# A four-layer streaming encoder step on one core: costs in the ordering table, side matmuls admitted some time after their estimate, and the rotated-key add moved from GpSimd to VectorE

## The chip, the cores and the metric

One core of one Trainium2 chip runs the whole program. Its engines each take their instructions in one fixed order: TensorE (PE in the profile, with PEld for its weight loads), VectorE (DVE), ScalarE (ACT), GpSimd (POOL) and SyncE (SP), which issues the transfers. The metric is the device time of one execution in microseconds, as the median over several runs.

## The reference

One inference step of a hybrid encoder for 256 frames of a new stream (prompt) and 64 frames of a running one (sample), so 320 columns of work in float32. Four layers in the pattern A, B, C, A:

- A: differential attention, 16 heads. Per head two softmax maps, `p = attn_map(q1, k1) - lam * attn_map(q2, k2)`, the output normalised, q and k rotated (rope). The sample frames also read 512 cached keys.
- B: sparse attention, where an indexer picks the 256 (or fewer) best keys of each query.
- C: RWKV-7 time mixing, a matrix state carried from token to token.

```
x <- x + W_out[i] (mixer(rmsnorm(x)) * silu(gate))
y = rmsnorm(x)
```

Returned beside y are the new keys and values of A and B, the index keys, and the states of C.

## The kernel before

All activations stand with the model dimension on the 128 partitions and the 320 frames along the free axis. Every projection is cut into tiles of 128 output columns; one tile is 48 matmuls of 320 columns: 16 pieces of the inner dimension, each in three products, because every float32 operand is split into two parts of a faster format (hi and lo). The weights come in by SP, are split into a ring of five slots by ACT (hi) and DVE (lo), and are multiplied into a PSUM bank. There are 307 such tiles, 14736 matmuls, called weight matmuls below; in the profile they carry `ring` in their names. The plan of tiles is fixed: layer A takes 64 (per head k, v, q and the gate of the head before), its output projection 16, then B and 16, C (v, two narrow tiles, k and r, then g) and 16, A and 16.

Everything else of a layer (rope, scores, softmax, transposes, products with the values, the recurrence of C) is side work. When a tile is done, a generator such as `on_k`, `on_q`, `attend`, `sample`, `steps` or `chain` is started for it and yields instructions in its own order. All generators, and the ring's `splitter`, are merged when the program is built into one order per engine. `Model` holds an estimated clock for each engine, `cost` gives each instruction an estimated length, and `ready` says when its inputs would be there. `pump` walks the generators and puts out the next instruction of each whose inputs are estimated to be ready by PE's estimated clock. Between any three weight matmuls (one inner piece) the loop at the end of the program calls `pump`, so a side matmul can be let in after each group of three. None of it runs on the chip: what is left is the order. On the chip an engine stops at an instruction whose inputs are late, and all that stands behind it on this engine stops too.

One head of layer A in steady state is four tiles, 192 weight matmuls, with these side groups on PE: the transposes of v (three), the scores of the prompt's rows (three products, from q and k), the scores of the sample (six) and of the last prompt rows (three) in split form, the transposes of the head before's output, those of the sample's map (five) and of the prompt's map (three, in `attend`, after eight exponentials on ACT and two combining instructions on DVE), and the eight products with the values. In `on_k` the rotated key is the sum of two DVE products `t1` and `t2`; the add stands at line 823 for A (32 heads in both layers) and 1278 for B (4), and the sum is stored, sent out, and split for the score products.

In layer C each of 16 tiles p has a `chain`: four prompt steps c0 to c3 (c4 is the sample's, beside them), each of three dependent groups of small matmuls with copies between them, then a normalisation over ACT, DVE and POOL, and three transposes. The result is operand number p of C's output projection, whose weight matmuls need all 16 from the 154th on.

Of the kernel before, what the change touches and what calls it, by code (L numbers as in the profile page):

```python
# [24 lines left out]
RING = 5  # L25
LEAD = 4
ARENA = 18480
NEG = -1.0e30


class Op:


    def __init__(self, eng, name, args, kw):
        self.eng, self.name, self.args, self.kw = eng, name, args, kw
        self.hold = not kw.get("stop", True)
        ins, outs = [], []
        for i, x in enumerate(args):
            if isinstance(x, bass.AP):
                (ins if i else outs).append(x)  # L40
        for k, x in kw.items():
            if isinstance(x, bass.AP):
                (outs if k in ("out", "accum_out") else ins).append(x)
        self.size = max([1] + [x.free_size() for x in ins + outs if name == "dma_start" or not _dram(x)])
        self.psum = any("psum" in x.name for x in ins)
        self.f32r = any(x.dtype == F32R for x in ins)
        self.width = outs[0].partition_size() if outs else 128
        self.bytes = outs[0].nbytes() if outs else 0
        self.run = min((run(x) for x in ins + outs), default=0) if name == "dma_start" else 0
        self.n = outs[0].free_size() if outs else 0  # L50
        self.scalars = sum(x.free_size() == 1 for x in ins) if self.n > 1 else 0
        self.accum = "accum_out" in kw
        self.ins = [region(x) for x in ins if "psum" not in x.name]
        self.outs = [region(x) for x in outs if "psum" not in x.name]
        self.banks = set()
        for x in ins + outs:
            if "psum" in x.name:
                a = int(x.offset) % int(x.ap[0][0])
                b = a + sum(int(st) * (int(n) - 1) for st, n in x.ap[1:])
                self.banks.update(range(a // 512, b // 512 + 1))  # L60
        self.column = int(outs[0].offset) // (outs[0].ap[0][0] or 1) if eng == "PE" else 0


def _dram(x):
    return str(x.space).endswith("DRAM")


def run(x):

    r = 1  # L70
    for st, n in reversed(x.ap if _dram(x) else x.ap[1:]):
        if n > 1 and st != r:
            break
        r *= int(n)
    return r
# [19 lines left out]
class Model:  # L95


    def __init__(self, engines):
        self.engines = engines
        self.clk = {e: 0.0 for e in engines}  # L100
        self.dma = self.hwdge = 0.0
        self.table = None
        self.mem, self.dram = {}, {}
        self.cols = {}
        self.bank = {}
# [27 lines left out]
    def cost(self, op):  # L133
        n = op.size
        if op.name == "dma_start":
            return 1040.0 if op.eng == "G" else 100.0
        if op.eng == "PE":
            n = op.n
            if op.column:
                return 27 if n <= 32 else 54  # L140
            if op.name == "transpose":
                return 0.84 * n
            if op.f32r:
                return 0.42 * n + 2
            return 1.67 * max(n, op.width) + 4
        if op.eng == "S":
            c = 0.714 * n + (90 if op.psum else 132) + 95 * op.scalars + 70 * op.accum
            f = op.args[2] if op.name == "activation" else None
            if f in (AF.Exp, AF.Tanh, AF.Sqrt):
                f = "sqrt" if f == AF.Sqrt else "exp"  # L150
                if f != self.table:
                    c += 1300
                    self.table = f
            return c
        if op.eng == "G":
            if op.kw.get("op") == OP.pow:
                return 165.0 * op.n + 300
            if op.name == "memset":
                return 0.835 * n + 35
            if op.name == "tensor_copy":  # L160
                return 3.33 * n + 120
            if op.name == "tensor_scalar":
                return 3.33 * n + 176 + 83 * op.scalars
            return 2.1 * n + 149
        if op.name == "reciprocal":
            return 6.45 * n + 69
        if op.name in ("tensor_scalar", "tensor_copy", "memset") and not op.psum:
            return 0.52 * n + 69 + 60 * op.scalars
        return 1.042 * n + 69 + 60 * op.scalars
# [38 lines left out]
class Sched:  # L208
# [45 lines left out]
    def pump(self):  # L254

        while True:
            self.moved, nxt = False, None
            for t in list(self.tasks):
                while self.settle(t):
                    n = 1  # L260
                    while t.queue[n - 1].hold:
                        n += 1
                    r = max(self.model.ready(op) for op in t.queue[:n])
                    if r > max(self.now, self.model.clk["PE"]):
                        nxt = r if nxt is None else min(nxt, r)
                        break
                    for op in t.queue[:n]:
                        self.model.emit(op)
                    del t.queue[:n]
                    self.moved = True  # L270
                    self.moves += 1
            if not self.moved:
                return nxt
# [164 lines left out]
def hybrid_kernel(ctx: ExitStack, tc: tile.TileContext, a, o, layers=DEPTH):  # L438
# [3 lines left out]
    PE, V, S, G, Q = [sched.engine(e) for e in ("PE", "V", "S", "G", "Q")]  # L442
# [27 lines left out]
    ring = wpool.tile([128, RING, 2, 512], F32R, name="ring")  # L470
    raw = wpool.tile([128, RAW, 2048], F32, name="raw")
    arena = wpool.tile([128, ARENA], F32, name="arena")
    psum = ppool.tile([128, 4096], F32, name="psum")
# [7 lines left out]
    class Layout:  # L481
# [3 lines left out]
        def ap(self, n):  # L485
            r = arena[:, self.off:self.off + n]
            self.off += n
            assert self.off <= ARENA, self.off
            return r
# [16 lines left out]
    def wait(*keys):  # L506
        while sched.cur.queue or not all(k in flags for k in keys):
            yield
# [220 lines left out]
    def layer_a(j, li, opn, opo, prev):  # L729
# [85 lines left out]
        def on_k(h):  # L815
            def gen(acc):
                yield from wait(("tab", li))
                t1, t2 = yield from TT.get(2)
                yield from rope_parts(t1.ap, t2.ap, acc.ap, cos, sin, 32)
                acc.rel()  # L820
                yield
                kr = yield from KR.get()
                G.tensor_add(kr.ap, t1.ap, t2.ap)
                t1.rel()
                t2.rel()
                flags["k", li, h] = kr
                Q.dma_start(o["new_a_k"][j, h], kr.ap)
                flags["kdone", li, h] = True
            return gen
# [245 lines left out]
    def layer_b(li, opn, opo, prev):  # L1075
# [153 lines left out]
        def topk():  # L1229
# [11 lines left out]
            yield from rounds(acc_p[:, 128:384], 8)  # L1241
            V.tensor_scalar(bias_p, acc_p, -2.5e38, NEG, op0=OP.is_ge, op1=OP.mult)
            flags["bias_p"] = True
            yield
            yield from rounds(acc_s[0:64], 18)
            V.tensor_scalar(bias_s[0:64], acc_s[0:64], -2.5e38, NEG, op0=OP.is_ge, op1=OP.mult)
            V.tensor_copy(bias_s[64:128], bias_s[0:64])
# [22 lines left out]
        def on_k(g):  # L1270
            def gen(acc):
                yield from wait(("tab", li))
                t1, t2 = yield from TT.get(2)
                yield from rope_parts(t1.ap, t2.ap, acc.ap, cosb, sinb, 64)
                acc.rel()
                yield
                kr = yield from KTT.get()
                G.tensor_add(kr.ap, t1.ap, t2.ap)
                t1.rel()
                t2.rel()  # L1280
                Q.dma_start(o["new_b_k"][g], kr.ap)
                flags["bk", g] = kr
            return gen
# [216 lines left out]
    def layer_c(li, opo, prev):  # L1500
# [18 lines left out]
        mts = {}  # L1519
        top = arena[:, ARENA - 2 * T:ARENA]  # L1520
        tw, ta = top[:, 0:T], top[:, T:2 * T]
# [8 lines left out]
        LL, XT, VS, VK = lv.slots(6, T), lv.slots(8, T), lv.slots(4, T), lv.slots(2, 640)  # L1530
        assert lv.off <= ARENA - 2 * T

# [106 lines left out]
        WL, VV = lk.slots(2, 512), lk.slots(2, T)  # L1639
        batch_at = ARENA - 2 * T - 2304  # L1640
        LG = Layout(batch_at - 4 * T).slots(4, T)
# [232 lines left out]
        SG = lg.slots(1, T)  # L1874
        assert ARENA - 2 * T <= lg.off - T and lg.off <= ARENA, lg.off
        SETS = Slots(sched, sets[0:3])
# [370 lines left out]
    for n, p in enumerate(pieces):  # L2247
# [13 lines left out]
        for i in range(4):  # L2261
# [6 lines left out]
            r = max(model.ready(x) for x in ops)  # L2268
            while True:
                nxt = sched.pump()  # L2270
                t = max(sched.now, model.clk["PE"])
# [127 lines left out]
```

## Time and profile before

| | us |
|---|---|
| median of 3 runs (2772.8 to 2778.11) | 2776.75 |
| the profiled execution | 2782.14 |
| its span, first to last instruction | 2780.3 |
| PE busy, of the span | 2702.5 |
| DVE / ACT / POOL busy | 1929.8 / 1466.2 / 467.0 |

PE is busy 97% of the span, but its records overlap (matmuls are pipelined), so the share hides short stops. A stop is read from the start times: the weight matmuls of a tile follow each other at a fixed pitch, and what lies between two of them beyond that pitch is side work or waiting. The profile puts nearly all instructions on line 198, the helper that emits them, so tiles and shapes tell them apart: `psum<-op_a,ring` or `psum<-op_b,ring` are weight matmuls, `psum<-cst,arena` are transposes, `psum<-arena` scores and products. An fp32 product of two arena operands has two records.

### The profile page before, as it was taken

The page shows a single profiled execution, that of the slowest core. Times are in us where ns is not written, and L with a number is a line of the kernel's source. Part 1 is how long each engine was busy: PE and PEld are TensorE (multiplying, and loading weights), DVE is VectorE, ACT ScalarE, POOL GpSimd, SP SyncE. Part 2 cuts the span into 40 slices and gives each one's busy share as a digit, 9 for nine tenths or more (in the row PEclk, how much of TensorE's full clock was granted, in tenths as well). Part 3 has the DMA queues.
Part 4 walks back from the last instruction along what each step waited for, and adds up shares of the span by engine and source line. Part 5 has one row for each costly group of instructions (what it writes and reads, how often), then busy time and mean ns, then how long its engine had stood idle before and what let it go on. Part 6 is the DMA issues. An engine that isn't in the chain of part 4 may idle for free.

```text
span 2780.3 us, 53272 instructions
## 1 busy us (share of the span) xinstructions
PE 2702.5 (97%) x19594; PEld 2573.0 (93%) x19594; DVE 1929.8 (69%) x4044; ACT 1466.2 (53%) x3582; POOL 467.0 (17%) x845
## 2 busy tenths in 40 slices
PE   7999999999999999989999999999999999999997
PEld 7999999999999999989999998888899999999997
DVE  7777777665799766458866667766656777777654
ACT  5655555554444544436544453667545555555553
POOL 3000000001000000022012635455311000000011
PEclk9999999999999999989999999999999999999999
DMA  6444444455434334565666676766454444444352
GB/s 219 150 143 142 141 143 145 141 173 187 142 127 149 119 131 140 189 175 180 228 180 203 172 206 174 256 219 196 149 193 149 146 146 146 147 145 148 131 174 104
DMA packets 219980, 455.23 MB, mean 164 GB/s; under 512 B 83270, under 2 KB 149254, under 8 KB 185798
## 3 DMA queue, kind: packets, MB, share of 16 engines
q1 hardware_dynamic: 219718, 451.83, 49.8%
q8 instruction: 154, 2.52, 0.4%
q14 instruction: 108, 0.88, 0.1%
HBM read 394.20 MB, written 57.55 MB: 162 GB/s over the span
## 4 chain that ended last, share of the span: by engine, by line
PE 44%; ACT 4%; DVE 3%; issue 2%; DMA 1%; POOL 0%; SPq 0%; DVEq 0%; ACTq 0%; POOLq 0%
PE psum L198 44%; ACT arena L198 3%; DVE arena L198 1%; DVE ring L198 1%; ACT ring L198 1%; DVE smt L198 1%; DMA arena<-yr_d 0%; DMA bv_d<-arena 0%; DMA arena<-l_d 0%; DVE op_a L198 0%; POOL arena L198 0%; DMA yr_d<-arena 0%; DMA v_d<-arena 0%; SPq L198 0%; DVE op_b L198 0%
## 5 line engine op out<-in xcount | busy, mean ns | idle before, releaser
L198 PE MATMUL psum<-op_a,ring 128*128 128x320 f32 x8496 | 1329.1, 313 | 20.3 <-ACT op_a L198 10.0
L198 PEld LDWEIGHTS psum<-op_a,ring 128*128 128x128 f32 x8496 | 1260.9, 189 | 34.9 <-ACT op_a L198 11.9
L198 DVE TENSOR_TENSOR ring<-raw,ring 128x512 fp32r<-128x512 f32 (+2 forms) x1228 | 856.8, 702 | 512.2 <-ACT ring L198 499.2
L198 ACT CAST ring<-raw 128x512 fp32r<-128x512 f32 (+2 forms) x1228 | 751.7, 618 | 834.1 <-PE psum L198 770.0
L198 PE MATMUL psum<-op_b,ring 128*128 128x320 f32 (+1 forms) x6240 | 996.6, 314 | 0.3 <-DVE ring L198 0.2
L198 PEld LDWEIGHTS psum<-op_b,ring 128*128 128x128 f32 (+1 forms) x6240 | 923.4, 188 | 17.4 <-issue 3.0
L198 DVE TENSOR_TENSOR arena<-psum,arena 32x320 f32<-32x320 f32 (+3 forms) x567 | 270.0, 476 | 82.7 <-PE psum L198 64.2
L198 PE MATMUL psum<-arena 128*64 128x64 f32 (+9 forms) x3428 | 302.7, 254 | 8.9 <-DVE arena L198 4.0
L198 PEld LDWEIGHTS psum<-arena 128*64 128x64 f32 (+4 forms) x3428 | 239.8, 147 | 63.8 <-issue 31.2
L198 POOL TENSOR_TENSOR arena<-arena 128x64 f32<-128x64 f32 (+18 forms) x254 | 179.6, 710 | 654.4 <-PE psum L198 240.4
L198 ACT COPY arena<-psum 64x128 f32<-64x128 f32 (+9 forms) x473 | 146.0, 332 | 133.5 <-PE psum L198 116.8
L198 ACT ACTIVATE arena<-psum,smt 64x576 f32<-64x576 f32 (+5 forms) x384 | 169.7, 443 | 72.4 <-PE psum L198 35.1
L198 PE MATMUL psum<-cst,arena 128*128 128x128 f32 (+3 forms) x807 | 133.0, 269 | 26.6 <-DVE arena L198 20.9
L198 PEld LDWEIGHTS psum<-cst,arena 128*128 128x128 f32 (+3 forms) x807 | 89.0, 135 | 65.2 <-issue 26.3
L198 POOL TENSOR_TENSOR smt<-smt,mhalf 128x3 f32<-128x3 f32 (+1 forms) x64 | 72.7, 1136 | 310.2 <-DVE smt L198 296.9
L198 POOL TENSOR_TENSOR ssum<-ssum,arena 128x320 f32<-128x320 f32 x70 | 64.6, 923 | 294.8 <-ACT arena L198 294.1
L198 POOL MEMSET smt<- 128x3 f32 (+2 forms) x85 | 8.3, 102 | 609.1 <-DVE smt L198 609.1
L198 ACT CAST op_b<-arena 128x320 fp32r<-128x320 f32 (+4 forms) x198 | 79.1, 417 | 49.3 <-DVE arena L198 27.1
L198 ACT ACTIVATE arena<-arena 128x320 f32<-128x320 f32 (+1 forms) x192 | 89.4, 473 | 29.0 <-DVE arena L198 17.6
L198 DVE TENSOR_TENSOR op_b<-arena,op_b 128x320 fp32r<-128x320 f32 (+4 forms) x198 | 91.7, 483 | 5.0 <-ACT op_b L198 4.8
L198 ACT CAST op_a<-arena 128x320 fp32r<-128x320 f32 (+2 forms) x136 | 59.3, 442 | 55.6 <-DVE arena L198 35.9
L198 DVE TENSOR_TENSOR arena<-arena 64x320 f32<-64x320 f32 (+13 forms) x207 | 83.8, 414 | 3.4 <-DMA arena<-l_d 0.5
(95 smaller groups left out, 1366.5 us busy)
## 6 DMA issues: line engine op xcount, KB each, us to landing
raw<-in_a_w_in_dram SPq DMA_DIRECT2D x120, 1024.0 KB, 5.0
raw<-in_c_w_rkvg_dram SPq DMA_DIRECT2D x52, 1024.0 KB, 5.4
raw<-in_w_out_dram SPq DMA_DIRECT2D x48, 1024.0 KB, 5.1
raw<-in_b_w_in_dram SPq DMA_DIRECT2D x45, 1024.0 KB, 4.9
raw<-in_w_out_dram SPq DMA_DIRECT2D x64, 256.0 KB, 3.6
arena<-rec_d SPq DMA_DIRECT2D x16, 962.5 KB, 5.2
raw<-in_c_w_rkvg_dram SPq DMA_DIRECT2D x48, 256.0 KB, 3.8
out_dram<-arena SPq DMA_DIRECT2D x72, 160.0 KB, 4.3
```

The costliest lines, as they stand in the source:

```text
L198: return getattr(self.engines[op.eng], op.name)(*op.args, **op.kw)
```

## The change

Five numbers or rules of the ordering, and two adds:

- ScalarE instructions with an accumulated sum are estimated 50 ns longer (120 for 70). GpSimd's power is estimated at 157 ns a column and 390 (165 and 300 before), its other two-input work at 2.3 ns a column (2.1).
- `SLACK`: `pump` treats a PE instruction of a generator as ready 400 ns after its estimate. Weight matmuls have no such addition.
- The rotated keys' add is issued on VectorE, in A and in B.
- `Op` and `Model` get some new fields that nothing reads.

```
+SLACK = 400.0
...
-            c = 0.714 * n + (90 if op.psum else 132) + 95 * op.scalars + 70 * op.accum
+            c = 0.714 * n + (90 if op.psum else 132) + 95 * op.scalars + 120 * op.accum
...
-                return 165.0 * op.n + 300
+                return 157.0 * op.n + 390
...
-            return 2.1 * n + 149
+            return 2.3 * n + 149
...
-                    r = max(self.model.ready(op) for op in t.queue[:n])
+                    r = max(self.model.ready(op) + (SLACK if op.eng == "PE" else 0.0) for op in t.queue[:n])
...
-                G.tensor_add(kr.ap, t1.ap, t2.ap)
+                V.tensor_add(kr.ap, t1.ap, t2.ap)
...
-                G.tensor_add(kr.ap, t1.ap, t2.ap)
+                V.tensor_add(kr.ap, t1.ap, t2.ap)
```

How it moves instructions is seen in the built order. First PE, in one steady head of the first layer A, from the sample's last transpose to the weight matmuls ahead of the next head's scores, before:

```order
L198 MATMUL psum<-cst,arena 64x64
L198 MATMUL psum<-op_a,ring 128x320 x24
L198 MATMUL psum<-cst,arena 128x128 x3
L198 MATMUL psum<-op_a,ring 128x320 x9
L198 MATMUL psum<-arena 128x128 x3
L198 MATMUL psum<-arena 64x128 x5
L198 MATMUL psum<-op_a,ring 128x320 x45
L198 MATMUL psum<-cst,arena 128x128 x2
L198 MATMUL psum<-cst,arena 64x128
L198 MATMUL psum<-op_a,ring 128x320 x72
```

And the same stretch in the changed kernel:

```order
L209 MATMUL psum<-cst,arena 64x64
L209 MATMUL psum<-op_a,ring 128x320 x27
L209 MATMUL psum<-cst,arena 128x128
L209 MATMUL psum<-op_a,ring 128x320 x3
L209 MATMUL psum<-cst,arena 128x128 x2
L209 MATMUL psum<-op_a,ring 128x320 x12
L209 MATMUL psum<-arena 128x128 x3
L209 MATMUL psum<-arena 64x128 x5
L209 MATMUL psum<-op_a,ring 128x320 x36
L209 MATMUL psum<-cst,arena 128x128 x2
L209 MATMUL psum<-cst,arena 64x128
L209 MATMUL psum<-op_a,ring 128x320 x72
```

The map's three transposes come after 27 weight matmuls (the first) and 30 (the other two) in place of 24, and the products with the values after 42 in place of 33. Counted from the program's start by the numbers behind the x, the transposes of v stand 12 weight matmuls into their tile (9 before), and the scores 36 (33 before).

Second PE, at the end of layer C, the last groups of chain 15 and what follows. Before: its step c3 (three groups), then its transposes:

```order
L198 MATMUL psum<-arena 64x64 x2
L198 MATMUL psum<-op_a,ring 128x320 x6
L198 MATMUL psum<-arena 64x64 x2
L198 MATMUL psum<-op_a,ring 128x320 x12
L198 MATMUL psum<-arena 64x64 x2
L198 MATMUL psum<-arena 64x128
L198 MATMUL psum<-arena 64x64 x2
L198 MATMUL psum<-op_a,ring 128x320 x57
L198 MATMUL psum<-cst,arena 128x128 x2
L198 MATMUL psum<-cst,arena 128x64
L198 MATMUL psum<-op_a,ring 128x320 x615
```

In the changed kernel c3 of chain 15 is one block (the second to the fourth row here); then come chain 14's transposes, three weight matmuls, and chain 15's transposes:

```order
L209 MATMUL psum<-op_a,ring 128x320 x18
L209 MATMUL psum<-arena 64x64 x6
L209 MATMUL psum<-arena 64x128
L209 MATMUL psum<-arena 64x64 x2
L209 MATMUL psum<-cst,arena 128x128 x2
L209 MATMUL psum<-cst,arena 128x64
L209 MATMUL psum<-op_a,ring 128x320 x3
L209 MATMUL psum<-cst,arena 128x128 x2
L209 MATMUL psum<-cst,arena 128x64
L209 MATMUL psum<-op_a,ring 128x320 x615
```

Chain 15's last step moved from 57 weight matmuls ahead of its transposes to 3 ahead of them.

Third VectorE, in the first layer A, from the split of the next cached keys on. Before, no row of these is the key's add (it stands on POOL):

```order
L198 TENSOR_TENSOR op_b<-arena,op_b 128x512
L198 TENSOR_TENSOR ring<-raw,ring 128x512
L198 TENSOR_TENSOR arena<-psum,arena 64x128
L198 TENSOR_TENSOR op_b<-arena,op_b 128x320
L198 TENSOR_TENSOR ring<-raw,ring 128x512
L198 TENSOR_SCALAR smt<-smt 128x3
L198 TENSOR_TENSOR ring<-raw,ring 128x512
L198 TENSOR_TENSOR arena<-psum,smt 128x256
L198 TENSOR_SCALAR arena<-arena,smt 64x128
L198 TENSOR_TENSOR arena<-psum,rstd 128x320
```

In the changed kernel:

```order
L209 TENSOR_TENSOR arena<-arena 128x320
L209 TENSOR_TENSOR op_b<-arena,op_b 128x512
L209 TENSOR_TENSOR ring<-raw,ring 128x512
L209 TENSOR_TENSOR arena<-psum,arena 64x128
L209 TENSOR_TENSOR op_b<-arena,op_b 128x320
L209 TENSOR_TENSOR ring<-raw,ring 128x512
L209 TENSOR_SCALAR smt<-smt 128x3
L209 TENSOR_TENSOR arena<-psum,rstd 128x320
L209 TENSOR_TENSOR ring<-raw,ring 128x512
L209 TENSOR_TENSOR arena<-psum,smt 128x256
```

The add is the first row, ahead of the cached keys' split; and the product that v's transposes read (`psum,rstd`) now stands ahead of the one that waits for POOL's power (`psum,smt`).

## Rows read from the trace of the kernel before

**Rows 1.** The page, part 1: busy time and share of each engine.
```profile
PE 2702.5 (97%) x19594; PEld 2573.0 (93%) x19594; DVE 1929.8 (69%) x4044; ACT 1466.2 (53%) x3582; POOL 467.0 (17%) x845
```

**Rows 2.** Stretches: length, busy PE, PEld, DVE, ACT, POOL, granted clock, DMA share, GB/s.
```profile
60.00:580.00 520.00, 510.15 (x3502) 483.11 (x3500) 375.38 (x820) 306.03 (x817) 39.96 (x91) 1.00 0.42 143
1480.00:1758.00 278.00, 267.51 (x1785) 254.15 (x1783) 190.20 (x334) 123.19 (x248) 127.27 (x194) 0.97 0.71 201
1758.00:1990.00 232.00, 230.91 (x2780) 192.26 (x2780) 158.78 (x372) 152.56 (x544) 123.24 (x259) 1.00 0.60 191
...
1987.00:1995.00 8.00, 6.09 (x30) 5.44 (x30) 4.53 (x8) 1.92 (x4) 0.93 (x2) 0.82 0.79 262
```

**Rows 3.** PE in order, one head of layer A: start, length, operation, count [idle before].
```profile
2200.02 10.80 PE L198 MATMUL psum<-op_b,ring 128*128 128x320 f32 x72
...
2211.64 0.73 PE L198 MATMUL psum<-op_b,ring 128*128 128x320 f32 x3
...
2213.01 2.36 PE L198 MATMUL psum<-op_b,ring 128*128 128x320 f32 x15
2215.21 0.52 PE L198 MATMUL psum<-op_a 128*128 128x256 f32 x3
...
2220.24 3.79 PE L198 MATMUL psum<-op_b,ring 128*128 128x320 f32 x24
2224.35 0.81 PE L198 MATMUL psum<-cst,arena 128*128 128x128 f32 x3 [0.32 <-DVE arena L198]
2224.91 1.56 PE L198 MATMUL psum<-op_b,ring 128*128 128x320 f32 x9
...
2228.02 6.86 PE L198 MATMUL psum<-op_b,ring 128*128 128x320 f32 x45
...
2235.23 10.07 PE L198 MATMUL psum<-op_b,ring 128*128 128x320 f32 x67
```

**Rows 4.** PE in order, where scores and transposes find their inputs ready.
```profile
2138.06 2.90 PE L198 MATMUL psum<-op_b,ring 128*128 128x320 f32 x18
...
2141.44 1.62 PE L198 MATMUL psum<-op_b,ring 128*128 128x320 f32 x9
...
2161.84 2.90 PE L198 MATMUL psum<-op_b,ring 128*128 128x320 f32 x18
...
2164.82 5.38 PE L198 MATMUL psum<-op_b,ring 128*128 128x320 f32 x35
```

**Rows 5.** DVE in order, same head, ahead of the map's transposes.
```profile
2222.06 0.18 DVE L198 RECIPROCAL smt<-smt 128x4 f32<-128x4 f32 x1 [2.43 <-ACT arena L198]
...
2223.85 0.74 DVE L198 SCALAR_TENSOR_TENSOR arena<-arena,smt 128x128 f32<-128x128 f32 x2
```

**Rows 6.** Groups by shape, 60 to 580 us, the last 760 to 1120: count, busy, mean ns.
```profile
L198 POOL TENSOR_TENSOR arena<-arena 128x320 f32<-128x320 f32 x14 | 16.8, 1202 | 115.5 <-ACT arena L198 44.6 <-PE psum L198 39.8 <-DVE arena L198 31.1
L198 DVE TENSOR_TENSOR arena<-arena 64x320 f32<-64x320 f32 x30 | 14.5, 483 | 0.5
L198 DVE TENSOR_TENSOR op_b<-arena,op_b 128x512 fp32r<-128x512 f32 x13 | 14.4, 1105 | 0.2 <-ACT op_b L198 0.2
...
L198 DVE TENSOR_TENSOR op_b<-arena,op_b 128x512 fp32r<-128x512 f32 x2 | 1.4, 689 | 0.0
```

**Rows 7.** PE in order, end of layer C.
```profile
1975.70 0.34 PE L198 MATMUL psum<-arena 128*64 128x64 f32 x4
...
1979.26 0.79 PE L198 MATMUL psum<-arena 128*64 128x64 f32 x10
1979.98 8.62 PE L198 MATMUL psum<-op_a,ring 128*128 128x320 f32 x57
1988.49 0.61 PE L198 MATMUL psum<-cst,arena 128*128 128x128 f32 x3
1990.89 9.37 PE L198 MATMUL psum<-op_a,ring 128*128 128x320 f32 x49 [1.79 <-ACT op_a L198]
```

**Rows 8.** DVE in order, chain 15's last product ahead of its transposes.
```profile
1987.11 1.24 DVE L198 TENSOR_TENSOR arena<-arena,smt 128x384 f32<-128x384 f32 x1 [0.35 <-POOL smt L198]
```

More of the change, by code (lines that the diff above doesn't have):

```diff
@@ L61, in __init__ @@
         self.column = int(outs[0].offset) // (outs[0].ap[0][0] or 1) if eng == "PE" else 0
+        self.mode = self.place = None
+        if eng == "PE":
+            self.mode = ins[0].partition_size() > 64, self.width > 64
+        elif outs and not _dram(outs[0]):
+            self.place = self.column if eng == "PE" else int(outs[0].offset) // (outs[0].ap[0][0] or 1), self.width
+        self.weights = any("ring" in x.name for x in ins)
+        self.pair = eng == "V" and not self.psum and sum(x.free_size() > 8 for x in ins) > 1
+        self.pool = eng == "G" and name.startswith("tensor_") and sum(x.free_size() > 32 for x in ins) > 1
 def _dram(x):
@@ L102, in __init__ @@
         self.table = None
+        self.last = {}
+        self.pool = (0.0, 0.0)
         self.mem, self.dram = {}, {}
```

## Prediction

> **What bounds the kernel now.** I read the busy shares first: PE is busy 97% of the span, no other engine over 69% [rows 1]. So time can only come from PE, and the question is how much of its busy time is work. The stretches by stage come next: PE is idle for 9.9 of 520 us in the first layer A, for 10.5 of 278 us in the second part of C, and for 1.1 of 232 us while C's chains run [rows 2]. Since a PE record also covers waiting inside it, I then read PE's order in time in one steady head of A and take differences of start times. Fifteen weight matmuls take 2215.21 - 2213.01 = 2.20 us, a pitch of 0.1467 us [rows 3]. A side group costs what lies between the weight matmuls around it beyond that pitch:
>
> - The map's transposes: 24 weight matmuls start at 2220.24, the next ones at 2224.91: 4.67 - 24 x 0.1467 = 1.15 us [rows 3].
> - The transposes of v: 45 from 2228.02, next at 2235.23: 7.21 - 6.60 = 0.61 us [rows 3].
> - The scores: 72 from 2200.02, next at 2211.64: 11.62 - 10.56 = 1.06 us [rows 3].
>
> The same groups cost less where their inputs are ready: three transposes 2164.82 - 2161.84 - 18 x 0.1467 = 0.34 us, the scores 2141.44 - 2138.06 - 2.64 = 0.74 us [rows 4]. So one head loses 0.81, 0.27 and 0.32 us, 1.40 of the 35.21 us from 2200.02 to 2235.23 [rows 3], though the view shows only 0.32 us of it as idle. Reading on through both layers, I find the first wait in 31 of the 32 heads, the second in 18, the third in 24.
>
> **The change, part by part.**
>
> *Later admission and longer estimates in A.* Side matmuls are let in 400 ns later, and PE's order has room for them only after every third weight matmul, 0.44 us. In the built order the transposes of v and the scores both move three weight matmuls into their tiles: 0.44 us later, more than their waits of 0.27 and 0.32. Both inputs come from DVE a fixed time after a weight tile ends, so both waits should go: 18 x 0.27 + 24 x 0.32 = 12.5 us.
>
> The map's transposes hang on the scores and move with them; against the scores the first moves by 3 weight matmuls (0.44 us), the others by 6 (0.88 us). What makes them late is ACT's eight exponentials with sums, where the estimate was short: DVE waits 2.43 us for ACT, and the second of two combining instructions ends at 2223.85 + 0.74 = 2224.59 [rows 5]. The first transpose started at 2224.35; without a wait it would have started about 0.5 us before (0.81 is shared between the first, waiting on the first instruction, and the other two). So the first may still be late by up to 0.3 us, by how DVE's ring splits fall beside it; I take 0.1 on average. The other two have 0.88 us against 0.81 and find their input. Splitting the group in two adds no work as far as I count. 31 x 0.81 = 25.1 us, less 31 x 0.1 = 3: 22 us.
>
> A next wait could be the products with the values, now 9 weight matmuls later against the tile. Their successors (norm, transposes of the output) run behind the next head's scores, far from PE. But DVE's reading of v stands behind the norm's first step on DVE, which now comes later too; its margin before v's transposes I work out at under 0.6 us. If it is gone, 0.27 us a head stays. Sum for A: 12.5 + 22 = 34.5, with the heads at a layer's start 35 us. Bounds: 37.6 + 3 if nothing waits any more, and 19 if the map's transposes keep half of their wait and v's all of it.
>
> *The add on VectorE.* 36 adds leave POOL, where one takes 1202 ns [rows 6]. On DVE the nearest row, the add of half as many partitions with the same columns, takes 483 ns [rows 6]: 36 x 0.48 = 17 us more DVE work, in stretches where DVE is busy 375 of 520 us [rows 2]; DVE's waits for the ring's free slots cover it. Nothing stands behind the add that its inputs delay, since they are DVE's own. The cached keys' split and the ring's next split stand behind it, and ring slots are filled two pieces ahead or more, some 3.5 us. Cost at PE: nothing, and 0.48 us a head (15 us) if that cover were gone. The key is ready about 0.8 us earlier; its readers are PE groups a tile later, so no gain.
>
> The rows say more on this: the split of 512 columns that runs beside POOL's add takes 1105 ns in A and 689 ns in B [rows 6]. The Trainium skill, SBUF — State Buffer, "Who interferes with whom", says why: a VectorE instruction with two SBUF inputs and a GpSimd instruction that reads SBUF use one read interface, and whichever comes second waits for the whole of the other. By that rule the move gives back about 1105 - 689 = 0.42 us of the 0.48; by plain load it costs 0.48. Neither reaches PE, so the sum does not use it.
>
> *C, second part.* Here chains of DVE and POOL steps feed PE, and single stops are long. Each dependent PE step moves by about as much as the step before it, so a wait shrinks by only 0.4 us where it is not the whole chain that is late. Bounds: all 10.5 us of idle gone, or as much again added; I take 2 us gained, near nothing, since POOL's queue and not the order makes most of these waits.
>
> *C, the chains.* PE has no idle time to win here (1.1 of 232 us [rows 2]), and every hop of the chain is let in 0.4 us later, so chains drift behind the weight stream. Before, step c3 of chain 15 starts at 1975.70, its last group at 1979.26; 57 weight matmuls fill 8.5 us, and the transposes start at 1988.49 with nothing to wait for [rows 7]. After, c3 is one block with no weight matmuls between its groups and three after it. From c3's last group to the transposes took 9.23 us [rows 7], an upper end for an unchanged path; of it PE now covers the group itself (0.79), chain 14's transposes (0.61) and three weight matmuls (0.44), so up to 7.4 us are idle. The lower end is about 1 us, if little more than the one product on DVE of 1.24 us [rows 8] were left. Many steps follow one another here, none faster for PE's waiting except for ring splits between them, so I take 6 us. The two hops inside the block add 1 us: the four dependent instructions of DVE and ACT behind the transposes leave PE 1.79 us idle [rows 7], 0.45 a step (0 to 2.6 for both, since 18 weight matmuls, 2.64 us, lay between them before). Then PE restarts at the lower clock: before, after 1.79 us of idle, 49 matmuls take 9.37 us where 49 x 0.1467 = 7.19 [rows 7], with a granted clock of 0.82 in that stretch [rows 2], a mix of 2.4 and 1.2 GHz. That cost 2.2 us after a short stop; I add 3 more for a long one (0 to 5). The Trainium skill, TensorE: Matmul & The Clock Gate, "Why this matters for your kernels", tells authors to leave no long pauses between bursts because the clock halves; this change makes such a pause, and the row shows the price at the smaller one. Term: +10 us, from +1 to +15.
>
> *Sum.* -35 - 2 + 10 = -27 us against the profiled execution of 2782.1 us (1.8 us more than its span): 2755. That execution lies 0.2% over the median of the runs, 2776.75; in their terms 2750 us.
>
> **The rivals.**
>
> 1. *The waits move with the groups.* All side groups go later together, so a group that waits for another side group gains little. For: the map's transposes hang on the scores. Against: they move three and six weight matmuls further than the scores. Then only the scores' 7.7 us, v's 4.9 and a third of 25 are won: -21 - 2 + 10 = -13, some 2764 us.
> 2. *All waits go and C's tail costs little:* -41 - 4 + 5 = -40, some 2737 us. For: the margins above are positive; ACT's and DVE's queues after PE's last weight matmul hold little but chain 15. Against: the first transpose's margin is near zero.
> 3. *Slower: C's chains become the bound.* Sixteen chains of 5 steps and 3 hops are 240 hops; a hop with no weight matmul beside it leaves PE waiting 0.45 us, as above. If the drift empties the weight stream beside the chains so that over 75 of the 240 stand uncovered, 34 us more are lost and the gain is eaten; at 110 it is -27 + 50 = +23 on 2782, some 2800 us in the terms of the runs. For: chain 15's block shows it happens at the end. Against: in the built order weight matmuls still lie between most groups until chain 14, and several chains interleave in one block.
> 4. *No change:* A gains 19, C's tail takes 15 and C's second part some: within 5 us of 2777.
>
> **How the numbers follow.** Forecast, 20 to 36 us faster (2741 to 2757): 0.55. Rival 1: 0.17. Rival 2: 0.15. Rival 4: 0.06. Rival 3: 0.07. What a measurement can tell is 0.2%, 5.5 us. Faster: 0.55 + 0.17 + 0.15 = 0.87; same 0.06; slower 0.07. The range reaches into rivals 1 and 2 by the same terms, with 5 us either way for C's second part: from 2737 - 5 = 2732 to 2764 + 5 = 2769.
>
> **What would show it.** The head of A should last 33.8 to 34.0 us for 35.21, with three transposes at 0.34 us and scores at 0.74; if the head lasts over 34.8, A's step is wrong. PE's idle ahead of chain 15's transposes should be 4 to 7 us with a lower clock behind it; if there is none, the tail's term is wrong. Stretches of B and of the output projections should keep their length within 1 us. POOL should lose some 43 us (36 x 1.2), DVE's split of 512 columns in A fall to about 0.7 us. If the chains' stretch grows by over 15 us, rival 3 holds.

## The result, and the profile of the changed kernel

The changed kernel takes 2739.07 us, median of 4 runs (2736.89 to 2740.95), against 2777.43 us for the kernel before in the same comparison: a ratio of 0.9865, 95% interval 0.9848 to 0.9882, so 38 us less. 2750 was forecast, in a range of 2732 to 2769. The profiled execution took 2740.95 us, its span 2739.1.

The page of the changed kernel, part 1, answers to [rows 1]:

```profile
PE 2677.7 (98%) x19594; PEld 2569.3 (94%) x19594; DVE 1926.6 (70%) x4080; ACT 1466.7 (54%) x3582; POOL 437.3 (16%) x809
```

PE executes the same 19594 matmuls and its share rises to 98%; DVE has 36 instructions more, POOL 36 fewer. The stretches by stage, columns as in [rows 2]: first layer A, C's second part, C's chains, and two pieces of 8 us at the end of the chains:

```profile
60.00:565.00 505.00, 504.93 (x3536) 487.79 (x3536) 376.38 (x840) 309.10 (x827) 28.48 (x78) 1.00 0.43 149
1455.00:1732.00 277.00, 263.98 (x1799) 251.28 (x1798) 189.02 (x332) 124.23 (x249) 130.11 (x193) 0.99 0.73 205
1732.00:1977.00 245.00, 237.54 (x2804) 197.68 (x2803) 163.51 (x382) 154.20 (x550) 126.97 (x262) 0.97 0.59 187
1958.00:1966.00 8.00, 4.23 (x34) 3.11 (x32) 5.24 (x12) 2.92 (x10) 3.17 (x5) 0.81 0.53 168
1966.00:1974.00 8.00, 4.31 (x12) 2.87 (x13) 4.04 (x8) 1.39 (x3) 2.33 (x2) 0.50 0.28 82
```

In A PE's idle time is gone: 0.07 us of 505, where it was 9.9 of 520. In the chains it has grown: 7.5 us of 245, nearly all of it in the last two rows, with a granted clock of 0.81 and 0.50 (0.50 is 1.2 GHz, 1.00 is 2.4). Before, the same weight matmuls (9600 to 10320, see below) had 1.9 us of it, the stop of 1.79 us in [rows 7].

Where the 41 us between the two profiled executions came from is read by the numbered weight matmuls: the same one is looked up in both traces, and the difference of its start times shows what was won up to there.

| stretch, weight matmuls | won or lost, us | forecast |
|---|---|---|
| first A, 0 to 3120 | -23.0 | |
| second A, 11040 to 14160 | -22.5 | both A: -35 |
| B and output projections | +0.5 | 0 |
| C up to the chains, 6960 to 9600 | -3.1 | -2 |
| C's chains, 9600 to 10320 | +7.1 | +10 |
| sum | -41.0 | -27 |

PE in order, one head of layer A in the changed kernel, columns as in [rows 3]:

```profile
2187.60 0.93 PE L209 MATMUL psum<-arena 128*128 128x64 f32 x6
...
2196.83 4.23 PE L209 MATMUL psum<-op_b,ring 128*128 128x320 f32 x27
2200.90 0.27 PE L209 MATMUL psum<-cst,arena 128*128 128x128 f32 x1
2200.93 0.69 PE L209 MATMUL psum<-op_b,ring 128*128 128x320 f32 x3
2201.45 0.38 PE L209 MATMUL psum<-cst,arena 128*128 128x128 f32 x2
2201.59 2.00 PE L209 MATMUL psum<-op_b,ring 128*128 128x320 f32 x12
...
2205.13 5.54 PE L209 MATMUL psum<-op_b,ring 128*128 128x320 f32 x36
2210.51 0.49 PE L209 MATMUL psum<-cst,arena 128*128 128x128 f32 x3
2210.76 10.80 PE L209 MATMUL psum<-op_b,ring 128*128 128x320 f32 x72
2221.40 0.33 PE L209 MATMUL psum<-arena 128*128 128x64 f32 x2
```

The head lasts 2221.40 - 2187.60 = 33.80 us from one head's scores to the next (35.21 before). By the forecast's own measure, the first map transpose costs 2200.93 - 2196.83 - 27 x 0.1467 = 0.14 us, the other two 2201.59 - 2200.93 - 0.44 = 0.22, v's three 2210.76 - 2205.13 - 5.28 = 0.35: 0.36 for the map against 1.15, 0.35 for v against 0.61. Nothing in the head waits.

DVE in order, the same head, ahead of the map's transposes:

```profile
2198.68 0.18 DVE L209 RECIPROCAL smt<-smt 128x4 f32<-128x4 f32 x1 [2.71 <-ACT arena L209]
2198.89 0.22 DVE L209 SCALAR_TENSOR_TENSOR smt<-smt,lamt 128x2 f32<-128x2 f32 x1
2199.32 0.69 DVE L209 TENSOR_TENSOR ring<-raw,ring 128x512 fp32r<-128x512 f32 x1 [0.21 <-ACT ring L209]
2199.93 0.74 DVE L209 SCALAR_TENSOR_TENSOR arena<-arena,smt 128x128 f32<-128x128 f32 x2
2200.59 0.48 DVE L209 TENSOR_TENSOR op_a<-arena,op_a 128x320 fp32r<-128x320 f32 x1
```

And before, the start of the scores on PE, and the split on DVE that lies between the two lines of [rows 5]:

```profile
2210.93 1.01 PE L198 MATMUL psum<-arena 128*128 128x64 f32 x6
```

```profile
2223.45 0.49 DVE L198 TENSOR_TENSOR op_a<-arena,op_a 128x320 fp32r<-128x320 f32 x1
```

The reciprocal comes 11.08 us after the scores' start, as before (2222.06 - 2210.93 = 11.13). But the split into `op_a` now stands behind the two combining instructions (`arena<-arena,smt`); before, it stood ahead of them. They end 2199.93 + 0.74 - 2187.60 = 13.07 us after the scores' start, before 2224.59 - 2210.93 = 13.66 [rows 5]. So ACT's path is not shorter; DVE's last part is, from 2.53 us to 1.99. Of these 0.54 us the `op_a` split makes up 0.40 (2223.45 to 2223.85).

DVE's groups in 60 to 565 us, the split and the moved add (before: [rows 6]):

```profile
L209 DVE TENSOR_TENSOR op_b<-arena,op_b 128x512 fp32r<-128x512 f32 x12 | 8.2, 684 | 0.0
...
L209 DVE TENSOR_TENSOR arena<-arena 128x320 f32<-128x320 f32 x14 | 6.8, 484 | 0.0
```

PE in order, the end of layer C (before: [rows 7]); the 10 matmuls at 1961.41 are the last group of chain 15's c3, then come the transposes of chain 14 and of chain 15:

```profile
1959.79 0.34 PE L209 MATMUL psum<-arena 128*64 128x64 f32 x4
1960.46 0.33 PE L209 MATMUL psum<-arena 64*64 64x64 f32 x4 [0.34 <-ACT arena L209]
1961.41 0.79 PE L209 MATMUL psum<-arena 128*64 128x64 f32 x10 [0.62 <-ACT arena L209]
1963.60 0.99 PE L209 MATMUL psum<-cst,arena 128*128 128x128 f32 x3 [1.40 <-DVE arena L209]
1966.37 1.48 PE L209 MATMUL psum<-op_a,ring 128*128 128x320 f32 x3 [1.79 <-ACT op_a L209]
1969.38 0.98 PE L209 MATMUL psum<-cst,arena 128*128 128x128 f32 x3 [1.53 <-DVE arena L209]
1972.15 13.08 PE L209 MATMUL psum<-op_a,ring 128*128 128x320 f32 x73 [1.79 <-ACT op_a L209]
```

From c3's last group to chain 15's transposes 7.97 us pass (9.23 before), with almost no work beside them: three stops, 1.40 + 1.79 + 1.53 = 4.7 us. The two hops ahead of it stop PE for 0.34 + 0.62 = 0.96 us more. The fourth long stop, 1.79 us behind chain 15's transposes, stood there before too [rows 7].

### The profile page after: what moved, and what is told of

It reads as the page before. It is cut to its first block, busy times and chain, and to the rows that moved or that the text cites. A ratio compares the mean times of both kernels' runs of the same rounds, so it can differ in the third digit from the quotient of the medians.

```text
span 2739.1 us, 53165 instructions
## 1 busy us (share of the span) xinstructions
PE 2677.7 (98%) x19594; PEld 2569.3 (94%) x19594; DVE 1926.6 (70%) x4080; ACT 1466.7 (54%) x3582; POOL 437.3 (16%) x809
## 4 chain that ended last, share of the span: by engine, by line
PE 51%; DVE 2%; DMA 1%; issue 1%; SPq 0%; POOL 0%; ACT 0%; DVEq 0%; POOLq 0%; ACTq 0%
PE psum L209 51%; DVE arena L209 1%; SPq L209 0%; DMA rec_d<-arena 0%; DVE ring L209 0%; DMA arena<-l_d 0%; DMA raw<-in_c_w_rkvg_dram 0%; DVE op_b L209 0%; POOL arena L209 0%; ACT ring L209 0%; POOL smt L209 0%; DVEq L2406 0%; DVE op_a L209 0%; ACT arena L209 0%; DVE smt L209 0%
## 5 line engine op out<-in xcount | busy, mean ns | idle before, releaser
L209 ACT COPY arena<-psum 128x256 f32<-128x256 f32 (+9 forms) x473 | 145.2, 331 | 95.4 <-PE psum L209 82.1
L209 ACT ACTIVATE arena<-psum,smt 64x128 f32<-64x128 f32 (+5 forms) x384 | 169.6, 442 | 25.5 <-DVE smt L209 15.8
L209 POOL TENSOR_TENSOR arena<-arena 128x64 f32<-128x64 f32 (+18 forms) x218 | 135.3, 624 | 38.8 <-DMA arena<-l_d 9.7
L209 DVE TENSOR_TENSOR arena<-arena 64x320 f32<-64x320 f32 (+13 forms) x243 | 100.0, 420 | 3.4 <-DMA arena<-l_d 0.6
L209 DVE TENSOR_TENSOR op_b<-arena,op_b 128x320 fp32r<-128x320 f32 (+4 forms) x198 | 85.9, 455 | 1.8 <-ACT op_b L209 1.6
```

Source lines behind the costliest of these rows:

```text
L209: return getattr(self.engines[op.eng], op.name)(*op.args, **op.kw)
```

## The experiments

In this section "waiting in A" is what the side groups of both layers (without the first four tiles) take beyond the cheapest groups of the same make, summed over all PE records: 47 us before, 3 in the changed kernel.

### One part of the change at a time

**s_only.** The kernel before, with

```
+SLACK = 400.0
...
+                    r = max(self.model.ready(op) + (SLACK if op.eng == "PE" else 0.0) for op in t.queue[:n])
```

> The kernel before with the 400 ns admission alone; costs and the add as before. Theory 1 (admission and longer estimates work only together): the scores move by 3 weight matmuls and lose their wait, but the map's transposes stand 66 weight matmuls behind the scores, as before, and keep about 0.8 us of waiting in 31 heads; C's tail gets the same late last chain as in the changed kernel. A -17, tail +7, so about 2767 us (2760 to 2772). Rival (the admission does it all): A -40 or more, 2738 to 2748 us, no waiting ahead of the map's transposes.

Measured: 2755.67 us, ratio 0.9924 (0.9909 to 0.9939). Between the two theories. Waiting in A 15 us; in the steady heads the scores are free, but 28 groups of three transposes still wait, most of them 0.3 us and not 0.8. PE in this kernel, from the sample's transposes to the map's:

```profile
2205.77 3.79 PE L199 MATMUL psum<-op_b,ring 128*128 128x320 f32 x24
2209.39 0.77 PE L199 MATMUL psum<-cst,arena 128*128 128x128 f32 x3
2209.91 2.00 PE L199 MATMUL psum<-op_b,ring 128*128 128x320 f32 x12
```

2209.91 - 2205.77 - 3.52 = 0.62 us, 0.28 of it waiting, though the transposes stand no further behind the scores than before. DVE's order explains it: here too the `op_a` split has gone behind the combining instructions, which end 13.07 us after the scores' start, as in the changed kernel. What the ordering moves on DVE counts as much as what it moves on PE.

**v_only.** The kernel before, in both places:

```
-                G.tensor_add(kr.ap, t1.ap, t2.ap)
+                V.tensor_add(kr.ap, t1.ap, t2.ap)
```

> The kernel before with the two adds on VectorE and nothing else. Theory 1: the transposes of v stand 3 weight matmuls later and lose their 0.27 us in 18 heads, all else stands where it stood: about 2772 us (2768 to 2776), DVE's split of 512 columns in A at 0.69 us. Rival A (the add lengthens DVE's path to PE by 0.48 us a head): 2785 to 2792 us. Rival B (freeing the read interface from GpSimd is itself worth much): 2755 to 2762 us.

Measured: 2764.41 us, 0.9954 (0.9939 to 0.9969): none of the three, between theory 1 and rival B. Waiting in A falls to 38 us: v's 5 as expected, and the scores' wait from 0.33 to 0.27 us a head, 3 in all. The rest lies in the start of the first head (1.6 us) and in B and C (3). DVE's split of 512 columns in A takes 685 ns, as theory 1 had it.

**c_only.** The kernel before, with the estimates alone:

```
-            c = 0.714 * n + (90 if op.psum else 132) + 95 * op.scalars + 70 * op.accum
+            c = 0.714 * n + (90 if op.psum else 132) + 95 * op.scalars + 120 * op.accum
...
-                return 165.0 * op.n + 300
+                return 157.0 * op.n + 390
...
-            return 2.1 * n + 149
+            return 2.3 * n + 149
```

> The kernel before with the longer estimates alone. Theory 1: the map's transposes stand 63 and 66 weight matmuls behind the scores, so they wait as before and the scores too; v's transposes move by 6 and stop waiting, -5; C's last chain ends 18 weight matmuls ahead of where its result is wanted, which takes away a stop of 1.8 us and the lower clock behind it, -4. About 2767 us (2762 to 2772). Rival (right estimates are what removes the waits): 2745 to 2755 us.

Measured: 2759.38 us, 0.9938 (0.9921 to 0.9955): 3 us faster than theory 1's range. Waiting in A 35 us, the scores' 13 unchanged; v's transposes wait 4 us less, near the 5 expected, and the map's 8 us less, which was not expected (most of them 0.70 us a time for 0.86). The chains' stretch is 5 us shorter, where 4 were expected.

**s0.** The changed kernel, with

```
-SLACK = 400.0
+SLACK = 0.0
```

> The changed kernel with the admission at 0 ns: the longer estimates and the add alone. Theory 1 (the waits that each takes away alone, 12 us by the estimates and 9 us by the add in layer A, are different ones and add up, so some 22 us of waiting stay in A over the kernel with the admission in A alone): 2748 to 2756 us. Rival (they are the same waits): 2757 to 2762 us. If the admission were not needed at all: 2729 to 2735 us.

Measured: 2748.56 us, 0.991 (0.9892 to 0.9929), theory 1; waiting in A 29 us, 26 more than with the admission: the scores 10, a single first map transpose in 24 heads 17.

**s_c.** The changed kernel, in both places:

```
-                V.tensor_add(kr.ap, t1.ap, t2.ap)
+                G.tensor_add(kr.ap, t1.ap, t2.ap)
```

> The changed kernel with the two adds back on GpSimd. PE's order of a head is the same as in the changed kernel. Theory 1 (once the admission is late, the add is worth nothing at PE, as the prediction's term of zero has it): same as the changed kernel within its noise, 2737 to 2743 us, no waiting in A over 5 us in all. Rival (the add keeps the 12 us that it is worth alone): 2748 to 2754 us, with the scores waiting again.

Measured: 2746.46 us, 0.9892 (0.9876 to 0.9909): again between the two; waiting in A 6 us. Against the changed kernel's profile 5.4 us are lost, 2.6 of them before weight matmul 720. In the steady heads the scores do not wait again; in four heads the map's second and third transposes wait 0.43 us. So the add is worth about 5 to 7 us beside the other parts, most of it at the layers' starts.

### The admission by place

**a_slack.** Each generator carries its own addition, 400 ns only if it belongs to layer A:

```
+        self.slack = SLACK if "layer_a" in name else 0.0
...
-                    r = max(self.model.ready(op) + (SLACK if op.eng == "PE" else 0.0) for op in t.queue[:n])
+                    r = max(self.model.ready(op) + (t.slack if op.eng == "PE" else 0.0) for op in t.queue[:n])
```

> The changed kernel with the 400 ns only for the generators of layer A, none in B and C. Theory 1 (A gives 45 us, the late admission costs about 10 in C's chains): same head as the changed kernel, C's last chain ends at weight matmul 10263 and not at the one that needs it (10281), no idle time of PE over 1 us there: 2726 to 2732 us. Rival (C's loss comes from the estimates or the add, not from the admission): 2736 to 2742 us, as the changed kernel.

Measured: 2730.94 us, 0.9834 (0.982 to 0.9849), theory 1: A as in the changed kernel, and 8 us less. PE in this kernel, chain 15's transposes are the last three:

```profile
1956.17 0.58 PE L209 MATMUL psum<-cst,arena 128*128 128x128 f32 x3
1956.68 7.30 PE L209 MATMUL psum<-op_a,ring 128*128 128x320 f32 x48
1963.82 0.61 PE L209 MATMUL psum<-cst,arena 128*128 128x128 f32 x3
1964.36 3.05 PE L209 MATMUL psum<-op_a,ring 128*128 128x320 f32 x19
```

48 weight matmuls lie ahead of them and none of the four stops is left. By the numbered weight matmuls the chains' stretch (9600 to 10320) takes 12.5 us less than in the changed kernel. The earlier part of C (6960 to 9600) takes 6.8 us more, but the order alone does not set this: in a_s800 below PE's order in C is the same as here, and the same part takes 2.0 us more than in the changed kernel.

**a_chain.** As a_slack, and for three generators of C too:

```
+        self.slack = SLACK if "layer_a" in name or name.split(".")[-1] in ("chain", "steps", "corners") else 0.0
```

> The admission of 400 ns for layer A and, of layer C, for the chains, their steps and their corners alone. Theory 1 (the hops of the chains add their 400 ns and the last chain comes late): the chains end as in the changed kernel, 2737 to 2742 us, PE idle over 1 us four times at the end of the chains. Rival (the loss comes from C's other generators): 2728 to 2733 us, as with layer A alone.

Measured: 2744.67 us, 0.989 (0.9871 to 0.9909); the same stops: theory 1, though 2.7 us above its range. The chains' own hops are enough to make the last chain late.

**nochain.** The reverse, 400 ns everywhere except in these three:

```
+        self.slack = 0.0 if name in ("chain", "steps", "corners") else SLACK
```

> The changed kernel with the 400 ns everywhere but for the chains of C, their steps and corners. Theory 1 (both the hops of the chains and C's earlier groups make the last chain late): the last chain still ends where its result is wanted, and the time is 2734 to 2742 us. Rival (the hops of the chains alone cost, and the late admission of C's earlier groups gains the 8 us by which the changed kernel beats layer A alone there): 2722 to 2729 us.

Measured: 2739.78 us, 0.9869 (0.9851 to 0.9887), theory 1: the last chain is late all the same, now with one long stop:

```profile
1961.62 0.56 PE L209 MATMUL psum<-op_a,ring 128*128 128x320 f32 x2 [0.53 <-DVE op_a L209]
1967.11 0.96 PE L209 MATMUL psum<-cst,arena 128*128 128x128 f32 x3 [4.94 <-DVE arena L209]
```

This is the stop of 4 to 7 us in one piece that the prediction expected of the changed kernel. So hops and earlier groups of C each make the last chain late by themselves.

### The size of the admission

**a_s200, a_s800.** a_slack, with

```
-SLACK = 400.0
+SLACK = 200.0
```

and with 800.0.

> Layer A alone, with 200 ns in place of 400. The scores stand where they stand with 400, but the map's transposes stand only 60 and 63 weight matmuls behind them (69 and 72 with 400; 66 before). Theory 1 (the waits follow the position): about 1 us of waiting ahead of the map's transposes in nearly every head, 30 us in all, 2756 to 2766 us. Rival (half the admission gives about half of the gain): 2738 to 2748 us.

> Layer A alone, with 800 ns in place of 400; the map's transposes and the scores stand another 3 weight matmuls later. Theory 1 (no wait is left to win, and the slack to the next use is wide): 2728 to 2734 us, as with 400. Rival (groups now come so late that their successors or the free slots wait): 2738 us or more.

Measured: 2732.35 us, 0.9841 (0.9823 to 0.986), and 2730.97 us, 0.9835 (0.982 to 0.985). With 800 it is theory 1. With 200 both theories fell: waiting in A is 4 us. The error was to take the path from the scores to the map as fixed. ACT, DVE and PE with 200 ns, from the scores on:

```profile
2216.11 0.62 ACT L209 CAST ring<-raw 128x512 fp32r<-128x512 f32 x1
```

```profile
2216.76 0.69 DVE L209 TENSOR_TENSOR ring<-raw,ring 128x512 fp32r<-128x512 f32 x1 [0.16 <-ACT ring L209]
2217.76 0.76 DVE L209 TENSOR_REDUCE smt<-psum 128x2 f32<-128x576 f32 x1 [0.31 <-PE psum L209]
...
2226.10 0.18 DVE L209 RECIPROCAL smt<-smt 128x4 f32<-128x4 f32 x1 [2.35 <-ACT arena L209]
```

```profile
2216.00 0.93 PE L209 MATMUL psum<-arena 128*128 128x64 f32 x6
2216.64 1.08 PE L209 MATMUL psum<-op_a 128*128 128x288 f32 x6
```

The reciprocal comes 2226.10 - 2216.00 = 10.10 us after the scores' start, 1.0 us sooner than before. In the kernel before, the same cast and the same row maxima, ACT and DVE:

```profile
2212.32 0.62 ACT L198 CAST ring<-raw 128x512 fp32r<-128x512 f32 x1 [1.21 <-PE psum L198]
```

```profile
2212.97 0.69 DVE L198 TENSOR_TENSOR ring<-raw,ring 128x512 fp32r<-128x512 f32 x1 [1.27 <-ACT ring L198]
2213.70 0.76 DVE L198 TENSOR_REDUCE smt<-psum 128x2 f32<-128x576 f32 x1
```

Before, ACT's cast into the ring waits 1.21 us for PE, DVE's ring split 1.27 for the cast, and the maxima stand behind it and start 2.77 us after the scores (1.76 with 200 ns). With 200 ns the scores of the sample also follow without weight matmuls between.

**lead3.** The kernel before, with the ring split three pieces ahead, so that no cast should wait for a slot:

```
-LEAD = 4
+LEAD = 3
```

> The kernel before with the ring's splits three pieces ahead of the matmuls in place of four; nothing else. Question: from the scores' start to the reciprocal on VectorE that ends the map's exponentials is 11.1 us before and 10.1 us with 200 ns in layer A. Theory 1 (before, ScalarE's cast into the ring waits for a slot that PE frees only behind the scores, VectorE's ring split waits for the cast, and the row maxima stand behind it): three pieces ahead the slot is free long before, and this path is 10.0 to 10.3 us. Rival (the path is set by the score products' own order): 11.0 to 11.2 us. The time is no test, since the scores and the map's transposes are also put 3 to 15 weight matmuls earlier: about 2780 to 2795 us by theory 1, 2800 to 2815 us by the rival.

Measured: 2769.33 us, 0.9973 (0.9964 to 0.9983); less than either theory said. Waiting in A is 34 us, 13 less than before, though the groups stand earlier. PE's scores, then DVE:

```profile
2197.27 1.01 PE L198 MATMUL psum<-arena 128*128 128x64 f32 x6
```

```profile
2199.11 0.76 DVE L198 TENSOR_REDUCE smt<-psum 128x2 f32<-128x576 f32 x1 [1.05 <-PE psum L198]
...
2207.69 0.18 DVE L198 RECIPROCAL smt<-smt 128x4 f32<-128x4 f32 x1 [3.04 <-ACT arena L198]
```

The maxima come 1.84 us after the scores and the reciprocal 10.42, just over theory 1's range and far from the rival's. So the ring split ahead of the maxima, which does not wait here, most likely made up most of the 1.0 us; the edit also moves other instructions of this path, and how the remaining 0.3 us arises is open.

**a8_lead3.** a_s800, with the same edit as lead3:

```
-LEAD = 4
+LEAD = 3
```

> The changed kernel with 800 ns for layer A alone and the ring's splits three pieces ahead. The last chain of C ends 39 weight matmuls ahead of where its result is wanted, and no cast waits for a slot. Theory 1 (what is left of waiting in C comes from engines that stand at a ring split): 2715 to 2726 us. Rival (the waits in C are those of its transfers and GpSimd): 2727 to 2734 us, as with four pieces ahead; with fewer pieces ahead than PE needs it would be slower, over 2740 us.

Measured: 2728.97 us, 0.9829 (0.9813 to 0.9844), the fastest of all but not told apart from layer A alone: the rival. Waiting in A is 0.4 us. C keeps stops of 2.67, 2.56 and 3.21 us between matmul starts.

## Why the prediction came out as it did

**Read rightly.** That PE's records hide the waits and that the pitch shows them; which three groups wait; that positions in PE's order take these waits away (with DVE's order, see below). The head lasts 33.80 us, at the edge of the 33.8 to 34.0 that were to show it. B and the output projections moved by 0.5 us in all. C's second part gave 3.1 us for 2, though this says little: a_slack, a_s200, a_s800, c_only and s0 have one and the same PE order there and take 518.7 to 524.0 us for it. The last chain comes late, at a clock that falls behind it: +7.1 us for +10. The stops between c3's last group and the transposes are 4.7 us for 6, in three pieces and not one, since chain 14's transposes had come late too; the two hops 0.96 us for 1; and some 1.4 us are left for the lower clock and all else, where 3 had been added. The chains' stretch grew by 7.1 us, so rival 3 (over 15) did not occur. The group that holds POOL's adds lost 44.3 us (179.6 to 135.3, 43 forecast), and the split fell to 684 ns.

**The mis-sized term: A, 35 forecast, 45.5 measured, over its own upper bound of 41.** (That bound is 37.6 + 3, and the 3 was given no working.) The mechanism held and the size did not. Four parts make up nearly all of the difference:

- The map's transposes gave 26.8 us for 22. The 31 waits averaged 0.86 us for 0.81 (in 10 heads the first transpose alone waited 0.93). And the 3 us that were held back for the first transpose were not needed: the prediction had named DVE's ring splits as what decides it, and DVE's order did move, in favour: 0.54 us, most of it from the `op_a` split that went behind the combining instructions.
- The scores gave 10.5 us for 7.7: 27 waited and not 24, and the three at the layers' starts waited longer, 0.5, 1.4 and 1.8 us. Three of them still do, 1.3 us in all.
- The scores of each layer's last two heads, which stand in one longer group with others, gave 1.4 us (four waits of 0.34), and the first four tiles of the program 2.0: the prediction took one steady head times the count and set 0.5 us for the starts.
- v's transposes gave 5.4 us for 4.9. Against all this, small gaps between weight matmuls grew by 1.4.

**The add, forecast at nothing.** In most steady heads that is right. At the layers' starts it is not: 5 to 7 us by s_c, in all. What was weighed there, that POOL's add holds up the split beside it, the traces bear out, and more sharply than the mean of 1105 ns in [rows 6] says. In the trace before, 8 of those 13 splits run beside the add and take 1367 to 1374 ns; the 5 others take 677 to 693. POOL and DVE in one such place:

```profile
163.93 1.23 POOL L198 TENSOR_TENSOR arena<-arena 128x320 f32<-128x320 f32 x1 [4.46 <-ACT arena L198]
```

```profile
164.34 1.37 DVE L198 TENSOR_TENSOR op_b<-arena,op_b 128x512 fp32r<-128x512 f32 x1
```

So on the mean 0.42 us came back for 0.48 spent (1105 to 684 ns). And s_c shows that the order decides which neighbour pays: with the add on POOL and the new order the same split took 681 ns, and a ring split beside the add, in most heads, about 1350 for 691, so that DVE's ring splits averaged 714 ns for 688.

**The rivals.** Rival 1 (waits move with the groups) fell: nothing moved on. Rival 2 named the time within 2 us, 2737, in part by luck: nearly all waits in A did go, as it said, but they gave 45.5 us and not 41, and the tail cost 7 and not 5. A cheap tail is what a_slack has, and it lands at 2731. s_only and c_only contradict the thought that the parts only work together: they give 21 and 18 us, the add 13; together 38, since what they take away in A overlaps and the admission costs in C.

**Open.** Whether the late admission gains anything in the earlier part of C is not shown. The changed kernel takes 517.2 us there and a_slack 524.0, but with a_slack's own PE order s0, a_s800 and c_only take 518.7 to 519.3. Whether a late admission there could be had without the late last chain was not tested either.

## What to carry to other kernels

Count a wait over all its occurrences, starts of stages included, before multiplying one steady period: here the period gave 35 us and the count 45. A safety margin in an ordering table belongs where a stage has weight work to put ahead of the group; in a chain of dependent steps each hop pays it again, so set it by stage (layer A alone gave 46 us, everywhere 38). And follow what the margin moves on the other engines: a split that stood ahead of the critical instruction decided as much as the position on PE. And before a few microseconds of a stage are put down to a change, look at runs with the same order there: here they differ by 5 us.

## What the runs showed of the hardware that had not been expected

GpSimd's small copies are as dependent on their neighbours as its adds: the copy of 64 x 1 took 268 ns on average before and 597 in the changed kernel (306 in v_only, 396 in s_c), so POOL's busy time fell by 29.7 us where its adds alone gave 44.3. The trace shows the neighbour: 20 of the 32 copies in the changed kernel begin 10 to 16 ns after one of VectorE's ring splits, end 38 to 41 ns after it, and take 717 to 721 ns. Before, 20 of them began 303 to 307 ns after another split (128x320), ended 38 to 41 ns after that, and took 217 to 220.

A queue can hide a stop that no compute engine's order shows. The changed kernel's longest stop in C lies between two weight matmuls; SP's issues, ACT and PE in order of time:

```profile
1693.46 11.03 SPq L209 DMA_DIRECT2D yr_d<-arena  x4
...
1710.92 0.59 SPq L209 DMA_DIRECT2D yr_d<-arena  x1
1711.60 0.86 SPq L209 DMA_DIRECT2D raw<-in_c_w_rkvg_dram  x2
...
1716.64 2.18 ACT L209 CAST ring<-raw 128x512 fp32r<-128x512 f32 x4 [7.53 <-DMA raw<-in_c_w_rkvg_dram]
...
1717.31 4.89 PE L209 MATMUL psum<-op_b,ring 128*128 128x320 f32 x21 [5.31 <-ACT ring L209]
```

The weights are issued behind stores of C's records and results on the same queue: four stores take it 11.03 us, and between 1692.45 and 1711.60 it issues no weights. ACT then waits 7.5 us for them, and PE 5.3. The kernel before has no stop over 0.4 us at this place; a_slack, a_s200, a_s800, c_only and s0, which have one PE order in C, stop there for 1.0 to 4.9 us. It is a part of what C could still give.
